# A hybrid decoder layer on one core: the sums of its twelve norms with ones as weights in four column groups, one filler and one split moved

## The chip, the core and the metric

The kernel runs on one core of one Trainium2 chip. Its time is the device time of one launch in microseconds (us), the median over runs. TensorE is called PE here, its weight loads PEld, VectorE DVE, ScalarE ACT, GpSimd POOL, and SyncE, which issues most of the transfers, SP.

## What is computed

One layer of a decoder for 1024 prompt tokens and 8 x 4 sample tokens, 1056 in all, with 1024 channels:

```python
def _rms(x, g):
    y = xf * lax.rsqrt(jnp.mean(xf * xf, axis=-1, keepdims=True) + EPS)
    return (y * g)

def _layer(x, p, ...):
    h = _rms(x, n_mix_pre)
    z = h @ w_in                       # q (8 heads x 64), k, v (2 x 64), u (4 x 128)
    a, k_state, v_state = attn_fn(q, k, v)         # 128 keys back, with sinks
    m, pool_state = _pool_mixer(u, pool_prev, pos0, w_pool, pool_scale)
    mix = jnp.concatenate([a, m], axis=-1) @ w_out
    x = x + _rms(mix, n_mix_post)
    f = _rms(x, n_ffn_pre)
    f = (jax.nn.silu(f @ w_gate) * (f @ w_up)) @ w_down
    x = x + _rms(f, n_ffn_post)
    x = x + jax.nn.sigmoid(x @ w_ple_gate) * (p @ w_ple)
    return x, k_state, v_state, pool_state
```

The eight results are the layer's output for prompt and sample, and the updated key, value and pooling buffers. All are float32.

## The kernel before, in words

Activations stand with channels on the 128 partitions and tokens along the free dimension. The 1056 tokens are cut into three groups (`g` = 0, 1, 2) of N = 352. A float32 product is made of three products in float32r: every operand is split into a high part (`hi`, a cast on ACT) and a rest (`lo`, a subtraction on DVE), by `split` (lines 172 to 174); `gemm` issues hi x hi, hi x lo and lo x hi for every 128 channels of the contraction. Nearly all matrix instructions come from one line, the helper `mm` (L128); `mt` (L122) turns a 128 x 128 block. Sums and scores are made in plain float32, which the trace shows as two records of PE for each instruction.

A norm needs, for each token, the sum of 1024 squares. DVE and ACT first add up eight channel blocks, so that `acc[g]`, 128 x 352, is left. `rstd_steps(acc)` (L355) then adds over the 128 partitions and spreads the result: PE sums (`b<-c,acc`), ACT takes the root (`sd`), DVE makes the reciprocal (L366), splits it into `hl` (L368, L369) and lays both parts into a tile `dg` (L375), and two products with a matrix of ones (`b<-dg,c`) bring 1/rms of all 352 tokens to all partitions. It runs twelve times: three norms at the start (`u_norm`), six in the channel sub-layer's input (`ffn_steps`, two for each group) and three in `x2_steps` near the end. The sums are three products, each with a 128-token piece of `acc` as weights and one column of ones as the moving side, the third piece overlapping the second. So token t stands on partition t mod 128 of column t // 128, and `diag`, three copies of the identity, puts it back in its place.

`yield a, b` in these steps hands over to the product stream: `turn` (L943) counts PE work, and a step goes on when the count has passed what it asked for (`a` divided by a share, plus `b`). At the start of the program the order on PE is fixed by hand (`pinned`), and the order on ACT and DVE in part (`fixed`); elsewhere the framework's scheduler orders each engine. [...]

The attention part mixes prompt and sample work (L890 to L922). `dscores` and `scores` make scores and their softmax (POOL multiplies by the reciprocal of the sum, L707), `dturned` turns the sample's weights in three banks, which ACT copies out (L818, L821), and `dvalues` multiplies them with the values. `filler(n)` takes n ready-made products of the output projection off a list, so that PE has work meanwhile; the first of them are `out_pool`, twelve matrix instructions and one ACT copy each (L844).

Late in the channel sub-layer `do_reload` (L1251) brings two tiles `fr` back from memory and splits them (`f_operand`), after waits of 50 and 70 in the count of `turn`.

Of the kernel before, what the change touches and what calls it, by code (L numbers as in the profile page):

```python
# [10 lines left out]
F32 = mybir.dt.float32  # L11
F32R = mybir.dt.float32r
AF = mybir.ActivationFunctionType
ALU = mybir.AluOpType
AX = mybir.AxisListType

P = 128
D = 1024
# [7 lines left out]
N = T // G  # L26
# [1 line left out]
OFF = tuple(N * g for g in range(G + 1))  # L28
NX = N

TB = 3
WIN = 128
NB = SEQ // WIN
PW = (2, 4, 8, 16)
# [28 lines left out]
def trunk_kernel(  # L63
# [33 lines left out]
    te, ve, se, ge = nc.tensor, nc.vector, nc.scalar, nc.gpsimd  # L97
# [4 lines left out]
    spool = ctx.enter_context(tc.tile_pool(name="spool", bufs=2))  # L102
# [5 lines left out]
    def nm(s):  # L108
        cnt[0] += 1
        return f"{s}{cnt[0]}"  # L110

    def act_tile(shape, dt=F32, s="a"):
        return apool.tile(shape, dt, tag="a", bufs=A_SLOTS, name=nm(s))

    def half(g, dt=F32, s="h"):
        return act_tile([P, 4, NS[g]], dt, s)
# [9 lines left out]
    def mm(*args, **kw):  # L126

        ins = te.matmul(*args, **kw)  # L128
        if pinned[0]:
            tc.keep_in_program_order(ins)  # L130

    def bank():
        return psum.tile([P, 512], F32, tag="b", name=nm("b"))
# [4 lines left out]
    def const(shape, src=None, s="c", dt=F32):  # L138
        t = cpool.tile(shape, dt, name=nm(s))
        if src is not None:  # L140
            nc.scalar.dma_start(t, src)
        return t
# [3 lines left out]
    ident = const([P, P])  # L146
    make_identity(nc, ident)

    diag = const([P, TB, P])
    lap = TB * P - N  # L150
    for i in range(TB - 1):
        ge.tensor_copy(diag[:, i, :], ident)
    ge.memset(diag[:, TB - 1, :], 0.0)
    ge.tensor_copy(diag[:, TB - 1, : P - lap], ident[:, lap:])
    ones = const([P, P])
    ge.memset(ones, 1.0)
    ones_r = const([P, P], dt=F32R)
# [1 line left out]
    epst = const([P, 1])  # L159
# [7 lines left out]
    def fix(ins):  # L167

        if fixed[0]:
            tc.keep_in_program_order(ins)  # L170
# [184 lines left out]
    def rstd_steps(acc):  # L355

        n = acc.shape[1]
        sm = bank()  # L360
        for i in range(TB):
            at = min(i * P, n - P)
            mm(sm[:, i : i + 1], acc[:, at : at + P], ones[:, 0:1], start=True, stop=True)
        sd = spool.tile([P, TB], F32, tag="sd", name=nm("sd"))
        fix(se.activation(sd, sm[:, :TB], AF.Sqrt, bias=epst, scale=1.0 / D))
        fix(ve.reciprocal(sd, sd))  # L366
        hl = spool.tile([P, 2, TB], F32R, tag="hl", name=nm("hl"))
        fix(ve.tensor_copy(hl[:, 0], sd))  # L368
        fix(ve.tensor_tensor(hl[:, 1], sd, hl[:, 0].bitcast(F32), op=ALU.subtract))  # L369
        dgs = []  # L370
        dg2 = act_tile([P, 2, TB, P], F32R, "dg")
        for h in range(2):
            dg = dg2[:, h]
            fix(
                ve.tensor_tensor(  # L375
                    dg, diag, hl[:, h].bitcast(F32).unsqueeze(2).to_broadcast([P, TB, P]), op=ALU.mult
                )
            )
            dgs.append(dg.rearrange("p i k -> p (i k)"))
        yield 6, 14  # L380
        ps = bank()
        for h in range(2):
            mm(ps[:, :n], ones_r, dgs[h][:, :n], start=h == 0, stop=h == 1)
        return ps[:, :n]

    def acc_rows():
        t = act_tile([P, 4, NX], s="acc")
        return [t[:, g, : NS[g]] for g in range(G)]
# [108 lines left out]
    n = 4 * NDEC * PST  # L497
# [51 lines left out]
    pinned[0] = True  # L549
    norms = [None] * G  # L550
    norms[0] = rstd_steps(acc1[0])
    for h in range(2):
        for c in range(4):
# [13 lines left out]
    for c in range(4):  # L567
        u_prod(c, 1, 1)
    norms[1] = rstd_steps(acc1[1])
    u_norm(norms[1], 1)  # L570
    for h in range(2):
# [4 lines left out]
    for c in range(4):  # L576
        u_evict(c, 1)
        se.copy(u_decode(c)[:, :, 0:PST], stt[:, c])
    split(wplh, wpll, wpl)
    norms[2] = rstd_steps(acc1[2])  # L580
    u_norm(norms[2], 2)
    for h in range(2):
# [42 lines left out]
    def project(i, j, g):  # L625
        ps = bank()
        gemm(ps[:, : NS[g]], ops8(weights(j), xs[g]))
        ve.tensor_tensor(qkv[i][:, OFF[g] : OFF[g + 1]], ps[:, : NS[g]], r1[g], op=ALU.mult)
# [17 lines left out]
    for c in range(4):  # L646
        n = NDEC * DSEQ
# [67 lines left out]
    def scores(b):  # L715


        t = act_tile([P, 8, WIN])
        nk = 2 * WIN if b else WIN
        lo = b * WIN + WIN - nk  # L720
        at = WIN * 4 // nk
        both = [[bank() for _ in range(4 // at)] for _ in range(2)]
        for c in range(4):
            for kv in range(2):
                rows = slice(64 * kv, 64 * kv + 64)
                i = c % at
                mm(
                    both[kv][c // at][:, i * nk : (i + 1) * nk],
                    qT[c][rows, b * WIN : (b + 1) * WIN],
                    kT[rows, lo : lo + nk],  # L730
                    start=True,
                    stop=True,
                )
        for kv in range(2):
            tk = t[:, 4 * kv : 4 * kv + 4, :]
            for i, ps in enumerate(both[kv]):
                tc_ = tk[:, i * at : (i + 1) * at, :]
                v = ps.rearrange("p (c k) -> p c k", k=nk)
                if b:
                    m = am[:, 0, :].unsqueeze(1).to_broadcast([P, at, WIN])  # L740
                    se.copy(tc_, v[:, :, :WIN])
                    ve.copy_predicated(tc_, m.bitcast(mybir.dt.int32), v[:, :, WIN:])
                else:
                    ve.tensor_tensor(tc_, v, m4(1), op=ALU.add)
            hs = slice(4 * kv, 4 * kv + 4)
            softmax(tk, 4, 0.125, skp[:, hs], nskp[:, hs])
        return t
# [62 lines left out]
    def dturned(t):  # L810
        pt = act_tile([P, NDEC + 1, P])
        for lo in (0, 4, 8):
            ps = bank()
            n = min(4, NDEC + 1 - lo)
            if lo < 8:
                for i in range(n):
                    mt(ps[:, i * P : (i + 1) * P], t[:, 0, (lo + i) * P : (lo + i + 1) * P])
                se.copy(pt[:, lo : lo + n, :], ps.rearrange("p (b c) -> p b c", c=P))  # L818
            else:
                mt(ps[: NDEC * DSEQ, :P], t[:, 0, 1024:])  # L820
                se.copy(pt[: NDEC * DSEQ, 8, :], ps[: NDEC * DSEQ, :P])  # L821
        return pt
# [23 lines left out]
    acc = acc_rows()  # L846
# [37 lines left out]
    def filler(n):  # L884
        for _ in range(n):
            if fill:
                f, *at = fill.pop(0)
                f(*at)
# [3 lines left out]
    td = dscores()  # L892
    t = scores(order[0])
    project(5, WQ[-1], 1)
    filler(1)
    od = bank()
    pts = [dturned(td[0])]
    filler(1)
    pts.append(dturned(td[1]))
    filler(1)  # L900
    ahead = scores(order[1])
    dvalues(pts, od)
    put(od, SEQ, NDEC * DSEQ)
# [52 lines left out]
    def chain(steps, wait=0, alone=False):  # L956

        chains.append([steps, now[0] + wait, alone])
# [46 lines left out]
    def f_operand(src, g):  # L1005
        hi, lo = half(g, F32R, "fh"), half(g, F32R, "fl")
        split(hi, lo, src)
        return hi, lo
# [242 lines left out]
    def do_reload():  # L1251
        def steps():
            ts = [half(2, s="fr") for h in range(2)]
            for h in range(2):
                nc.sync.dma_start(ts[h], fsd[h])
            yield 0, 50
            for h in range(2):
                fs[2][h] = f_operand(ts[h], 2)
                yield 10, 70

        chain(steps())

# [219 lines left out]
```

## Time and profile before

| what | before |
|---|---|
| median of 3 runs | 1089.85 us (1087.95 to 1090.51) |
| the profiled execution's own time | 1088.29 us |
| its span, first to last instruction | 1086.5 us |
| granted TensorE clock | 0.999 |
| PE busy | 1076.8 us (99%) |
| DVE, ACT, POOL busy | 873.2 (80%), 512.4 (47%), 283.2 us (26%) |

Busy times of PE are modelled from a pipeline: the records of two successive matrix instructions overlap, so the distance from start to start tells what one costs. In rows of the timeline the first number is the start in us, the second the time from the start of the first of the merged instructions to the end of the last; the shapes stand as rows*columns of the array in use, then partitions x elements of the moving side.

### The profile page before, as it was taken

The numbers are of one execution on the slowest core, as the hardware profiler recorded it, in microseconds if no ns is written. First come the engines' busy times: TensorE is split into PE (matmuls) and PEld (weight loads), VectorE is DVE, ScalarE is ACT, GpSimd is POOL, SyncE is SP. The second block draws the span as 40 slices with busy tenths as digits, with TensorE's granted clock in tenths as the row PEclk, the third lists the DMA queues.
The fourth block names the chain that finished last, engine by engine and source line by source line (L and its number), as shares of the span: only waits on it lengthen the run. The fifth ranks groups of instructions, "written<-read, shape, count | busy, mean of one in ns | idle before, by whom it ended". The sixth has DMA issues, their size and how long they took to land.

```text
span 1086.5 us, 17727 instructions
## 1 busy us (share of the span) xinstructions
PE 1076.8 (99%) x6867; PEld 1060.1 (98%) x6867; DVE 873.2 (80%) x1312; ACT 512.4 (47%) x877; POOL 283.2 (26%) x212
## 2 busy tenths in 40 slices
PE   9999999999999999999999999999999999999998
PEld 8999988899999999999999999999998999999998
DVE  6777478886878956796598898898899997969973
ACT  7423277774555533345543343443344365545531
POOL 0073032200000023436545445454442000022300
PEclk9999999999999999999999999999999999999999
DMA  8121311534553432322222222212234556553461
GB/s 296 59 72 39 120 50 40 188 143 141 190 184 130 136 117 78 131 78 78 78 79 78 83 74 85 91 59 97 79 112 161 170 179 224 182 210 125 135 203 60
DMA packets 43572, 131.27 MB, mean 121 GB/s; under 512 B 5060, under 2 KB 15588, under 8 KB 43488
## 3 DMA queue, kind: packets, MB, share of 16 engines
q1 hardware_dynamic: 42160, 128.38, 34.7%
q10 hardware_dynamic: 1328, 1.77, 0.5%
q8 instruction: 54, 0.88, 0.3%
q14 instruction: 30, 0.25, 0.1%
HBM read 114.25 MB, written 15.87 MB: 120 GB/s over the span
## 4 chain that ended last, share of the span: by engine, by line
PE 95%; DVE 3%; POOL 1%; ACT 1%; issue 1%; DMA 0%; SPq 0%; DVEq 0%; POOLq 0%; ACTq 0%
PE b L128 94%; PE b L122 1%; POOL wr L1058 1%; DVE sl L174 1%; DMA xr<-in_x_dram 0%; DVE hp L174 0%; DVE a L805 0%; DVE ap L1228 0%; ACT a L701 0%; DVE wl L174 0%; DVE hf L1133 0%; POOL a L707 0%; DVE w L174 0%; ACT sh L173 0%; DVE fl L174 0%
## 5 line engine op out<-in xcount | busy, mean ns | idle before, releaser
L1058 POOL TENSOR_TENSOR wr<-wr,wr 128x512 f32<-128x512 f32 x108 | 174.0, 1625 | 482.2 <-DMA wr<-in_w_gu_dram 242.3
L173 ACT CAST wh<-wr 128x1024 fp32r<-128x1024 f32 (+1 forms) x138 | 142.1, 1031 | 164.3 <-PE b L128 92.2
L174 DVE TENSOR_TENSOR wl<-wr,wh 128x1024 fp32r<-128x1024 f32 (+1 forms) x138 | 168.1, 1219 | 51.4 <-ACT wh L173 35.4
L128 PE MATMUL b<-fh,wh 128*128 128x352 f32 x624 | 201.5, 323 | 0.0
L128 PE MATMUL b<-fh,wl 128*128 128x352 f32 x624 | 200.0, 320 | 0.0
L128 PE MATMUL b<-fl,wh 128*128 128x352 f32 x624 | 199.9, 320 | 0.0
L173 ACT CAST sh<-wr 128x1024 fp32r<-128x1024 f32 x72 | 75.7, 1051 | 138.0 <-POOL wr L1058 131.9
L128 PE MATMUL b<-fh,sh 128*128 128x352 f32 x416 | 134.3, 323 | 0.0
L128 PE MATMUL b<-fl,sh 128*128 128x352 f32 x416 | 133.2, 320 | 0.0
L128 PE MATMUL b<-fh,sl 128*128 128x352 f32 x416 | 133.2, 320 | 0.0
L174 DVE TENSOR_TENSOR sl<-wr,sh 128x1024 fp32r<-128x1024 f32 x72 | 97.5, 1356 | 36.1 <-ACT sh L173 18.2
L128 PEld LDWEIGHTS b<-fl,wh 128*128 128x128 f32 x624 | 117.4, 188 | 0.0
L128 PEld LDWEIGHTS b<-fh,wh 128*128 128x128 f32 x624 | 117.0, 188 | 0.0
L128 PEld LDWEIGHTS b<-fh,wl 128*128 128x128 f32 x624 | 116.9, 187 | 0.0
L128 PE MATMUL b<-h,wh 128*128 128x352 f32 x480 | 105.6, 326 | 0.6 <-ACT h L426 0.6
L128 PE MATMUL b<-hid,wh 128*128 128x352 f32 x416 | 99.6, 322 | 0.0
L128 PEld LDWEIGHTS b<-h,wh 128*128 128x128 f32 x480 | 82.4, 190 | 1.6 <-ACT h L426 0.9
L1058 POOL TENSOR_TENSOR wr<-wr 128x512 f32<-128x512 f32 x36 | 51.0, 1416 | 105.9 <-DVE w L174 105.9
L128 PEld LDWEIGHTS b<-fl,sh 128*128 128x128 f32 x416 | 78.2, 188 | 0.0
L128 PEld LDWEIGHTS b<-fh,sh 128*128 128x128 f32 x416 | 78.0, 188 | 0.0
L128 PEld LDWEIGHTS b<-fh,sl 128*128 128x128 f32 x416 | 77.9, 187 | 0.0
L128 PE MATMUL b<-hp,sh 128*128 128x352 f32 x320 | 76.7, 322 | 0.8 <-DVE p L1085 0.6
(195 smaller groups left out, 2245.7 us busy)
## 6 DMA issues: line engine op xcount, KB each, us to landing
wr<-in_w_gu_dram SPq DMA_DIRECT2D x88, 512.0 KB, 3.3
wr<-in_w_dn_dram SPq DMA_DIRECT2D x40, 512.0 KB, 3.2
wr<-in_w_pg_dram SPq DMA_DIRECT2D x16, 512.0 KB, 3.5
x<-in_x_dram SPq DMA_DIRECT2D x6, 704.0 KB, 9.9
x1d<-x SPq DMA_DIRECT2D x6, 704.0 KB, 3.6
x<-x1d SPq DMA_DIRECT2D x6, 704.0 KB, 5.7
out_y_dram<-yo SPq DMA_DIRECT2D x24, 176.0 KB, 1.9
wr<-in_w_out_b_dram SPq DMA_DIRECT2D x8, 512.0 KB, 3.3
```

The costliest lines, as they stand in the source:

```text
L122: ins = te.transpose(out, src, ident)
L128: ins = te.matmul(*args, **kw)
L173: fix(se.copy(hi, src))
L174: fix(ve.tensor_tensor(lo, src, hi.bitcast(F32), op=ALU.subtract))
L1058: ge.tensor_tensor(out, a, b, op=op)
```

## The change

Three edits.

1. In `rstd_steps` the roles are swapped. The weights are now 32 columns of ones, and `acc` moves, in four pieces of w = 88 tokens; piece j goes to columns 32j to 32j+31 of the array, so its sums stand on partitions 32j to 32j+31 of PSUM, 88 of them in each row. Root, reciprocal and split work on 88 elements a partition, where there were 3. `dg` is the product of `lead` (one on partition 32j of column j, else zero), spread over 88 elements, with the 88 values, spread over four pieces: 352 elements where there were 384. POOL makes `lead` with four copies of one column, where it cleared and filled `diag`.
2. One `filler(1)` that stood behind the second `dturned` stands ahead of the first.
3. The waits in `do_reload` are 90 and 30, where they were 50 and 70.

```diff
-    diag = const([P, TB, P])
-    lap = TB * P - N
...
+    lead = const([P, 4])
+    for j in range(4):
+        ge.tensor_copy(lead[:, j : j + 1], ident[:, 32 * j : 32 * j + 1])
...
         n = acc.shape[1]
+        w = n // 4
         sm = bank()
-        for i in range(TB):
-            at = min(i * P, n - P)
-            mm(sm[:, i : i + 1], acc[:, at : at + P], ones[:, 0:1], start=True, stop=True)
-        sd = spool.tile([P, TB], F32, tag="sd", name=nm("sd"))
-        fix(se.activation(sd, sm[:, :TB], AF.Sqrt, bias=epst, scale=1.0 / D))
+        for j in range(4):
+            mm(sm[32 * j : 32 * j + 32, :w], ones[:, :32], acc[:, j * w : (j + 1) * w], start=True, stop=True)
+        sd = spool.tile([P, w], F32, tag="sd", name=nm("sd"))
+        fix(se.activation(sd, sm[:, :w], AF.Sqrt, bias=epst, scale=1.0 / D))
         fix(ve.reciprocal(sd, sd))
-        hl = spool.tile([P, 2, TB], F32R, tag="hl", name=nm("hl"))
+        hl = spool.tile([P, 2, w], F32R, tag="hl", name=nm("hl"))
...
-        dg2 = act_tile([P, 2, TB, P], F32R, "dg")
+        dg2 = act_tile([P, 2, 4, w], F32R, "dg")
+        at_row = lead.unsqueeze(2).to_broadcast([P, 4, w])
         for h in range(2):
             dg = dg2[:, h]
-            fix(
-                ve.tensor_tensor(
-                    dg, diag, hl[:, h].bitcast(F32).unsqueeze(2).to_broadcast([P, TB, P]), op=ALU.mult
-                )
-            )
+            part = hl[:, h].bitcast(F32).unsqueeze(1).to_broadcast([P, 4, w])
+            fix(ve.tensor_tensor(dg, at_row, part, op=ALU.mult))
...
     project(5, WQ[-1], 1)
-    filler(1)
+    filler(2)
     od = bank()
     pts = [dturned(td[0])]
     filler(1)
     pts.append(dturned(td[1]))
-    filler(1)
     ahead = scores(order[1])
     dvalues(pts, od)
...
-            yield 0, 50
+            yield 0, 90
             for h in range(2):
                 fs[2][h] = f_operand(ts[h], 2)
-                yield 10, 70
+                yield 10, 30
```

Lines stand one to seven places earlier in the changed kernel (L844 is L838 there, L818 is L812).

The first place is ACT in the attention part, from the copy of the first filler's result (`y`, from PSUM bank `b`) on; 32x128 and 128x512 are the copies of the turned blocks into `a`, and `wh` is the cast of the next weights. Before:

```order
L844 COPY y_1287<-b_1443 128x352
L698 ACTIVATE es_1406<-es_1406 128x4
L701 ACTIVATE a_1366,sm_1409<-a_1366,nmx_1404 128x128 x4
L818 COPY a_1458<-b_1459 128x512
L818 COPY a_1458<-b_1465 128x512
L821 COPY a_1458<-b_1471 32x128
L844 COPY y_1287<-b_1474 128x352
L818 COPY a_1488<-b_1489 128x512
L818 COPY a_1488<-b_1495 128x512
L821 COPY a_1488<-b_1501 32x128
L173 CAST wh_1918<-wr_1225 128x1024
L844 COPY y_1285<-b_1504 128x352
```

The same place on ACT in the changed kernel:

```order
L838 COPY y_1290<-b_1446 128x352
L692 ACTIVATE es_1409<-es_1409 128x4
L695 ACTIVATE a_1369,sm_1412<-a_1369,nmx_1407 128x128 x4
L838 COPY y_1290<-b_1460 128x352
L169 CAST wh_1921<-wr_1228 128x1024
L812 COPY a_1475<-b_1476 128x512
L812 COPY a_1475<-b_1482 128x512
L815 COPY a_1475<-b_1488 32x128
L838 COPY y_1288<-b_1491 128x352
L812 COPY a_1505<-b_1506 128x512
L812 COPY a_1505<-b_1512 128x512
L815 COPY a_1505<-b_1518 32x128
```

A second copy of a filler and the cast of the weights now stand ahead of all copies of the turned blocks; the last of these, the smaller of 32x128, moves from ahead of the cast to the end of the group. The same instructions are in both.

The second place is DVE at the fourth norm, the first of `ffn_steps`, from the reciprocal on (`y_1286` and `y_1289` are the sum of the two halves of the output projection, which waits for a product of PE). Before:

```order
L366 RECIPROCAL sd_2524<-sd_2524 128x3
L368 CAST hl_2527<-sd_2524 128x3
L863 TENSOR_TENSOR y_1286<-y_1286,b_2533 128x352
L369 TENSOR_TENSOR hl_2527<-sd_2524,hl_2527 128x3
L375 TENSOR_TENSOR dg_2530<-c_82,hl_2527 128x384 x2
```

And in the changed kernel:

```order
L362 RECIPROCAL sd_2528<-sd_2528 128x88
L857 TENSOR_TENSOR y_1289<-y_1289,b_2537 128x352
L364 CAST hl_2531<-sd_2528 128x88
L365 TENSOR_TENSOR hl_2531<-sd_2528,hl_2531 128x88
L372 TENSOR_TENSOR dg_2534<-c_82,hl_2531 128x352 x2
```

Here the sum `y` moved ahead of the cast, so that three steps of the norm stand behind it where two did.

For the third edit neither ACT nor DVE nor SP has an instruction in another place: the casts `fh<-fr` are the 595th and 602nd rows of ACT in both. Behind the last norm, some thirty instructions of DVE and a dozen of ACT swap places with their neighbours.

More of the change, by code (lines that the diff above doesn't have):

```diff
@@ L29 @@
 NX = N
-TB = 3
 WIN = 128
@@ L147, in trunk_kernel @@
     make_identity(nc, ident)
-    diag = const([P, TB, P])
-    lap = TB * P - N
[L151 to L154, printed above, removed]
+    lead = const([P, 4])
+    for j in range(4):
+        ge.tensor_copy(lead[:, j : j + 1], ident[:, 32 * j : 32 * j + 1])
     ones = const([P, P])
```

## The prediction

> **What bounds the kernel now.** I read the page first: busy time by engine (part 1) and the chain that ended last (part 4).
>
> ```profile
> PE 1076.8 (99%) x6867; PEld 1060.1 (98%) x6867; DVE 873.2 (80%) x1312; ACT 512.4 (47%) x877; POOL 283.2 (26%) x212
> PE 95%; DVE 3%; POOL 1%; ACT 1%; issue 1%; DMA 0%; SPq 0%; DVEq 0%; POOLq 0%; ACTq 0%
> ```
>
> PE is dense and makes up 95% of the chain. So what PE issues less, or waits less, comes off the time one for one; work of DVE, ACT or POOL counts only where PE waits for it. Next, the waits of PE, where two rows matter here:
>
> ```profile
> PE b L128 <- DVE ap L1228: 1.7, 2, 1.5
> PE b L122 <- POOL a L707: 1.1, 1, 1.1
> ```
>
> The second is the place that the moved filler touches. The first is the largest wait for DVE, late in the channel sub-layer; the order of no engine changes there.
>
> **The sums on PE, what goes.** The timeline of the first norm on PE, with its neighbours:
>
> ```profile
> 25.24 0.72 PE L128 MATMUL b<-c,acc 128*128 128x1 f32 x6
> 25.82 1.53 PE L128 MATMUL b<-h,wh 128*128 128x352 f32 x8
> 27.19 0.81 PE L128 MATMUL b<-h,wl 128*128 128x352 f32 x4
> 28.15 1.44 PE L128 MATMUL b<-h,wh 128*128 128x352 f32 x8
> ```
>
> The row at 28.15 gives the pace of a product undisturbed: eight records in 1.44 us, the last lasting 0.32, so (1.44 - 0.32) / 7 = 0.16 us. From 25.24 to 27.19 stand the six records of the sums and eight such products: 1.95 - 8 x 0.16 = **0.67 us** for one norm. One column streams in no time; it is the weights, 128 columns for each record, that cost. Two norms follow each other directly:
>
> ```profile
> 274.02 1.39 PE L128 MATMUL b<-c,acc 128*128 128x1 f32 x12
> 275.52 0.32 PE L128 MATMUL b<-fl,wh 128*128 128x352 f32 x1
> ```
>
> One product stands between these two rows, so the pair costs 1.50 - 0.16 = 1.34 us.
>
> **What comes.** No 32-column groups stand in the trace of before, but 64-column groups (128*64) and halves of the rows (64*128) do, in the attention part:
>
> ```profile
> 132.43 0.81 PE L128 MATMUL b<-a,a 64*128 64x256 f32 x6
> 132.87 0.38 PE L128 MATMUL b<-a,a 64*128 64x256 f32 x2
> 133.18 0.43 PE L128 MATMUL b<-h,wh 128*128 128x352 f32 x1
> 133.18 0.30 PEld L128 LDWEIGHTS b<-h,wh 128*128 128x128 f32 x2 [0.33 <-DVE a L805]
> 148.49 1.01 PEld L128 LDWEIGHTS b<-a,a 128*64 128x64 f32 x32 [0.17 <-issue]
> 181.53 0.74 PE L128 MATMUL b<-a,a 128*64 128x512 f32 x2
> ```
>
> - Stream: three pairs of 256 columns start in 0.81 - 0.38 = 0.43 us, 0.215 a pair, 0.84 ns a column. 88 columns take 0.074 us, two records 0.148.
> - Changing the cut of the array: the last pair of 256 starts at 132.87 and streams until 133.085, but the full product starts at 133.18, 0.09 us later. A norm now pays this twice, in and out. [...]
> - Weights after such a change are loaded in the open: the second load starts at 133.18 + 0.30 - 0.19 = 133.29, so 0.11 us for 128 columns. For 32 columns I take 0.03 by proportion.
> - Groups beside each other: 32 loads of 64 columns take 1.01 us, 0.03 each, where one of 64 would take 0.055 by the same proportion, so two groups load at once. And two records of 512 columns are over in 0.74, which one behind the other would need 2 x 512 x 0.84 ns = 0.86 for streaming alone. So groups overlap. How far apart they start has two bounds: nearly nothing (the paired loads), or a group's two loads, 0.054 for 32 columns, three times over: 0.16. I take 0.02, by the 32 loads, which are the longer series.
>
> One norm: 0.09 + 0.03 + 0.148 + 0.02 + 0.09 + 0.11 = **0.49 us**, so 0.18 saved (0.04 at the other bound). The pair shares its changes of cut: 0.49 + 0.148 = 0.64, so 0.70 saved.
>
> **What the longer chain does.** Behind the sums stand one step of ACT and three small ones of DVE, now with 88 elements. The price of size, from the groups of instructions:
>
> ```profile
> L1085 DVE TENSOR_TENSOR p<-p,b 128x352 f32<-128x352 f32 x78 | 40.1, 514 | 13.2 <-PE b L128 12.6
> L1178 ACT ACTIVATE sl<-b 128x352 f32<-128x352 f32 x22 | 10.1, 457 | 3.0 <-PE b L128 3.0
> L365 ACT ACTIVATE sd<-b,c 128x3 f32<-128x3 f32 x12 | 3.1, 262 | 3.6 <-PE b L128 3.3
> L697 DVE TENSOR_TENSOR es<-c,nmx 128x4 f32<-128x4 f32 (+1 forms) x18 | 2.6, 153 | 0.1
> ```
>
> DVE: (514 - 153) / 348 = 1.04 ns an element, so 85 more cost 0.09 us in each step, 0.27 in three; the two `dg` lose 32 elements each, 0.07. ACT: (457 - 262) / 349 = 0.56 ns, so 0.05. The bounds: nothing at all if small steps are all fixed cost, or this. I take this, since these are the same instructions in the two sizes. PE waits for the result only where it has no other work; before, that happened once by over 0.1 us, at the third norm (49.29 below). Three norms are close:
>
> ```profile
> 24.66 1.38 ACT L436 ACTIVATE xr<-xr 128x1408 f32<-128x1408 f32 x1 [1.97 <-DVE h L428]
> 26.00 0.26 ACT L365 ACTIVATE sd<-b,c 128x3 f32<-128x3 f32 x1
> 26.79 1.02 DVE L375 TENSOR_TENSOR dg<-c,hl 128x384 fp32r<-128x384 f32 x2
> 27.67 0.38 PEld L128 LDWEIGHTS b<-dg,c 128*128 128x128 f32 x2
> 47.73 0.16 DVE L366 RECIPROCAL sd<-sd 128x3 f32<-128x3 f32 x1
> 49.29 0.19 PEld L128 LDWEIGHTS b<-dg,c 128*128 128x128 f32 x1 [0.19 <-DVE dg L375]
> 227.06 0.52 DVE L863 TENSOR_TENSOR y<-y,b 128x352 f32<-128x352 f32 x1 [1.38 <-PE b L128]
> 227.57 1.02 DVE L375 TENSOR_TENSOR dg<-c,hl 128x384 fp32r<-128x384 f32 x2
> 228.63 0.35 PEld L128 LDWEIGHTS b<-dg,c 128*128 128x128 f32 x2
> ```
>
> First norm: `sd` cannot start earlier, since ACT is busy with the squares until 26.0. The second `dg` ended at 27.81 and its load started at 27.67 + 0.38 - 0.19 = 27.86; now it ends 0.05 + 0.27 - 0.07 = 0.25 later and the load is in the open. PE loses **0.21 us** here (0.25 + 0.11 of load, less the 0.14 that lay between load and product), whatever the sums save. Third norm: DVE is behind (the reciprocal starts at 47.73, PE already waits), so the 0.27 - 0.07 = **0.20** comes straight on top. Fourth norm: the cast now stands behind `y`, which PE releases 0.18 earlier; `dg` then ends at 227.57 + 1.02 - 0.18 + 0.20 (the cast's place) + 0.20 (size) - 0.07 = 228.74, the load stays at 228.63 + 0.35 - 0.19 = 228.79, and the 0.18 is lost: **0**. At the other seven single norms and the pair I count the whole saving: 7 x 0.18 + 0.70 = **1.96 us**. The cover there is the products up to `b<-dg,c`; where it is gone, a norm is worth about 0.
>
> **The filler.** The stretch in question, from several engines' timelines:
>
> ```profile
> 138.84 0.32 PE L128 MATMUL b<-mh,wl 128*128 128x352 f32 x1
> 140.25 0.33 PE L122 MATMUL b<-c,a 128*128 128x128 f32 x1 [1.08 <-POOL a L707]
> 144.69 1.05 ACT L818 COPY a<-b 128x512 f32<-128x512 f32 x2
> 145.63 0.25 ACT L821 COPY a<-b 32x128 f32<-32x128 f32 x1
> 145.79 0.44 ACT L844 COPY y<-b 128x352 f32<-128x352 f32 x1
> 148.54 1.15 ACT L741 COPY a<-b 128x256 f32<-128x256 f32 x4
> 148.12 0.19 PEld L128 LDWEIGHTS b<-a,a 32*64 32x64 f32 x4 [0.33 <-issue]
> 149.53 0.43 PE L128 MATMUL b<-mh,wh 128*128 128x352 f32 x1
> ```
>
> PE stood from 138.84 + 0.16 to 140.25, 1.25 us. The moved filler, 12 x 0.16 = 1.92 us, fills this. But ACT, not PE, is late next: from 144.69 to 148.54 it goes without a pause through the copies of both turned tiles, two fillers' copies and the cast of weights, and all it does before hangs on POOL and DVE, not on PE. In the new order the same work lies in the same 3.85 us, with the last small copy of the turned blocks at its end: it starts at 148.54 - 0.16 (the distance of the small copy at 145.63 to its successor) = 148.38 and ends at 148.63. `dvalues` needs it. Before, its first products started together at 148.12; now the second of them starts at about 148.69, and the part up to 149.53, 1.41 us, moves to end at 150.09: **0.56 us lost**. Nothing later gives it back, since PE has no other wait in that part. The bounds are that and a gain of 1.25.
>
> **The rest.** `lead` for `diag` spares POOL work in the first 3 us, before PE has data: 0. The waits in `do_reload`: the order stays, 0. DVE's swaps behind the last norm stand where PE never waits: 0, at the price of a rival below.
>
> Sum: -1.96 + 0.21 + 0.20 + 0 + 0.56 = **-0.99 us**. The profiled execution took 1088.29 (span 1086.5), so it would take 1087.3. The median of the runs shown is 1.56 above that execution; I set the change against the median: 1089.85 - 0.99, **1088.9 us**, with its own range 1087.8 to 1090.1 (the upper end with 0.14 less saved at each of the seven and the pair).
>
> **Rivals.**
> 1. *The column groups run one after another* (the slower side). Then eight records stream for 8 x 0.074 = 0.59: a norm costs 0.09 + 0.03 + 0.59 + 0.09 + 0.11 = 0.91, 0.24 more than before; the pair 1.50, 0.16 more. With 7 x 0.24 + 0.16 + 0.32 (first norm: its sums now end 0.1 later) + 0.35 + 0.24 + 0.56 = 3.3 the time is 1093.1. It decides as soon as less than a third of the streams overlap. Against it: the rows at 148.49 and 181.53. [...] The row at 148.49, two column groups at once, disagrees for 64 columns; no run here shows 32.
> 2. *The filler does fill the gap*, because ACT gets to the copies earlier than its old timeline says: then -1.25 in place of +0.56, 1087.0 to 1087.1. For it: ACT's start at 144.69 follows steps of DVE stretched while POOL works, which may fall otherwise. Against: none of their order changes.
> 3. *The small steps hardly grow*: no stall at the three norms, each saves 0.18 but the third, which stays: -1.96 - 0.36 + 0.56 = -1.76, 1088.1.
> 4. *An eviction comes late behind the last norm*, where DVE's order changed. The nearest price is the wait for `ap` above, 1.5 to 1.7: 1090.5.
>
> **How the numbers follow.** Forecast 0.48, rivals 0.12, 0.22, 0.08, 0.10. About 0.2%, 2.2 us, is what a measurement of this kernel can tell from no change: faster is under 1087.7, slower over 1092.0. Faster: most of rival 2 (0.20) and the low ends of forecast and rival 3 (0.08). Slower: rival 1 and a little of rival 4: 0.15. The rest, 0.57, is the same. The range reaches from 1086.7, below rival 2, to 1091.5, above rival 4, and leaves rival 1 out.
>
> **What would show it.** In the timeline, four groups of 32 whose eight records end within 0.25 us of the first, and 0.49 between the products around them; if 0.9, rival 1. Loads of `dg` waiting at the first and third norm by 0.2 and 0.4. At about 139 to 141 no wait for POOL, and at 145 to 149 waits of PE for ACT's copies, the next filler starting near 150.1 less what is saved ahead; if near 148.3, rival 2. A wait of PE behind 1000 would be rival 4. I would be wrong altogether if DVE's place in the stretch with `ap` shifted.

## The result, and the profile after

The changed kernel takes **1092.37 us** (median of 12 runs, 1090.77 to 1095.51) against 1088.86 us of before (12 runs beside them, one of which took 3789.48 us; a median does not feel it): ratio 1.0034, 95% interval 1.0026 to 1.0042. It is slower by 3.5 us. The forecast was 1.0 us faster, the range ended at 1091.5. The forecast of 1088.9 was set against the median of three runs, 1089.85; with twelve, before itself takes what was forecast for after.

The profiled execution of after took 1091.78, its span is 1090.0. First the busy times on its page:

```profile
PE 1079.7 (99%) x6891; PEld 1058.0 (97%) x6891; DVE 878.9 (81%) x1312; ACT 512.9 (47%) x877; POOL 281.8 (26%) x212
```

PE is idle for 1090.0 - 1079.7 = 10.3 us, before for 1086.5 - 1076.8 = 9.7. So of the 3.5 us only 0.6 are waits. The rest stands in PE's busy time, although the twelve sums became cheaper. The place shows in the busy times by stretch, here one stretch of 120 us in the channel sub-layer, first of before, then of after (columns: PE busy and its records, then PEld, DVE, ACT, POOL, the granted clock, the share of the transfers):

```profile
460.00:580.00 120.00, 120.00 (x757) 120.00 (x756) 95.07 (x120) 59.41 (x95) 56.67 (x35) 1.00 0.24 80
```

```profile
460.00:580.00 120.00, 120.00 (x752) 120.00 (x751) 94.35 (x119) 59.98 (x96) 54.05 (x35) 1.00 0.24 80
```

PE never pauses in either, the clock is full in both, all its work there is full products of 352 columns, and yet it gets through five fewer. A record lasts two starts, so about two more reach into the window: 120 / 755 = 0.1589 us a product before, 120 / 750 = 0.1600 after. The starts in the two traces show it sharper: six products (a period after which the distances repeat) take 953.3 ns in before and 960.0 in after, from 340 to 817 us, without a drift. That is 3.33 us in this stretch alone.

Before has a slower stretch of its own, behind the reloads, and its own trace tells:

```profile
842.00:876.00 34.00, 34.00 (x213) 34.00 (x212) 32.45 (x47) 15.35 (x26) 0.00 (x0) 1.00 0.49 166
342.00:376.00 34.00, 34.00 (x216) 34.00 (x215) 33.00 (x37) 18.66 (x22) 0.00 (x0) 1.00 0.42 140
```

34 / 211 = 0.1611 us a product against 34 / 214 = 0.1589. There are three steady **rhythms** of dense products: 953, 960 and 967 ns for six. In the traces of before and after PE changes from one to another only where the series of products is broken: by a wait, by the sums, or by a few products of the same size that read other tiles. So it goes in both at the products of the pooling mixer (`b<-mh,a`, nine at a time): 967 ns before the first nine (at 80.5 us in before), 960 behind them, 953 behind the second nine (at 93.4 us).

Now the places that the change touches. The sums, at the first norm and at the pair, from the timeline of PE in after:

```profile
25.02 0.36 PE L127 MATMUL b<-acc,c 128*32 128x88 f32 x8
25.31 1.55 PE L127 MATMUL b<-h,wh 128*128 128x352 f32 x8
...
274.76 0.32 PE L127 MATMUL b<-fh,wl 128*128 128x352 f32 x1
275.01 0.51 PE L127 MATMUL b<-acc,c 128*32 128x88 f32 x16
275.46 0.43 PE L127 MATMUL b<-fh,wh 128*128 128x352 f32 x1
275.72 0.32 PE L127 MATMUL b<-fl,wh 128*128 128x352 f32 x1
```

Eight records are over in 0.36 us: the four groups run beside each other. The pair costs 275.72 - 274.76 - 2 x 0.16 = 0.64 us.

The small steps behind them at the third norm, from the timelines of DVE and PE in after; then the groups of reciprocals (instructions, busy time, mean ns of one), of after and of before:

```profile
48.01 0.69 DVE L362 RECIPROCAL sd<-sd 128x88 f32<-128x88 f32 x1
48.73 0.20 DVE L364 CAST hl<-sd 128x88 fp32r<-128x88 f32 x1
48.97 0.25 DVE L365 TENSOR_TENSOR hl<-sd,hl 128x88 fp32r<-128x88 f32 x1
49.14 0.95 DVE L372 TENSOR_TENSOR dg<-c,hl 128x352 fp32r<-128x352 f32 x2
49.81 0.77 PE L127 MATMUL b<-dg,c 128*128 128x352 f32 x2 [0.48 <-ACT wh L169]
```

```profile
L362 DVE RECIPROCAL sd<-sd 128x88 f32<-128x88 f32 x12 | 8.2, 693 | 2.2 <-ACT sd L361 2.2
```

```profile
L366 DVE RECIPROCAL sd<-sd 128x3 f32<-128x3 f32 x12 | 1.9, 169 | 2.6 <-ACT sd L365 2.6
```

The reciprocal costs (693 - 169) / 85 = 6.2 ns an element, six times what I charged; the cast costs next to nothing more (medians 205 ns for 88 elements and 169 for 3). PE waits for `dg` at 49.81 (the row names ACT's cast, on which these products do not depend; the first of the two `dg` is done about half-way through the 0.95 us from 49.14).

What PE waits for in after, by line (us in total, times, the longest), and then the stretch of the moved filler on PE:

```profile
PE b L127 <- DVE ap L1221: 1.7, 2, 1.5
PE b L127 <- DVE dg L372: 0.9, 2, 0.5
PE b L127 <- ACT a L812: 0.7, 1, 0.7
PE b L127 <- ACT y L838: 0.3, 1, 0.3
```

```profile
146.10 0.70 PE L127 MATMUL b<-a,a 64*128 64x256 f32 x2 [0.29 <-ACT y L838]
147.52 3.55 PE L127 MATMUL b<-a,a 64*128 64x256 f32 x50 [0.73 <-ACT a L812]
151.00 0.43 PE L127 MATMUL b<-mh,wh 128*128 128x352 f32 x1
```

The wait for POOL's `a` is gone, and two waits for ACT's copies stand in its place.

Product by product, the starts in after against those in before give the account (us; a plus is lost):

| place | forecast | measured |
|---|---|---|
| up to the first norm (start of the program) | 0 | -0.30 (+0.37 in a second execution) |
| first norm | +0.21 | +0.76 (+0.38 in a second execution) |
| third norm | +0.20 | +0.59 |
| seven single norms, sums | -1.26 | -1.31 |
| pair | -0.70 | -0.69 |
| fourth norm | 0 | -0.13 |
| filler | +0.56 | +0.17 |
| tenth norm (first of `x2_steps`; the expectations below call it the seventh single norm), wait for dg | 0 | +0.92 |
| reloads and waits for `p` and `ap`, 817 to 840 us | 0 | -0.32 |
| rhythm, 340 to 817 us | not thought of | +3.33 |
| rhythm, 840 to 875, 910 to 995, behind the last norm | not thought of | -0.47, +0.55, +0.55 |
| sum (whole shift 3.5) | -0.99 | +3.65 |

Not in the table are a slower rhythm of after between 229 and 274 us, +0.24, and the products right behind several norms, -0.03 to -0.10 each; with these the account comes to the 3.5. Without the four rhythm terms, 3.96 us together, the change would be worth -0.3 to -0.5 us: no change. Of these terms only +3.33 and the +0.55 between 910 and 995 us came in a second execution of both kernels as well; the others differ between executions of one program (see the end).

### The profile page after: what moved, and what is told of

Its sections match the earlier page's. It is cut to its first block, busy times and chain, and to the rows that moved or that the text cites. A ratio compares the mean times of both kernels' runs of the same rounds, so it can differ in the third digit from the quotient of the medians.

```text
span 1090.0 us, 17775 instructions
## 1 busy us (share of the span) xinstructions
PE 1079.7 (99%) x6891; PEld 1058.0 (97%) x6891; DVE 878.9 (81%) x1312; ACT 512.9 (47%) x877; POOL 281.8 (26%) x212
## 4 chain that ended last, share of the span: by engine, by line
PE 87%; DVE 7%; DMA 2%; issue 2%; ACT 1%; POOL 0%; SPq 0%; DVEq 0%; ACTq 0%; POOLq 0%
PE b L127 86%; DVE wl L170 1%; DMA xr<-in_x_dram 1%; PE b L121 1%; DVE ap L1221 1%; DVE ap L1228 1%; DMA a<-in_p_dram 1%; DVE sl L170 1%; POOL wr L1051 0%; DVE acc L848 0%; DVE hp L170 0%; DMA c<-in_gains_dram 0%; ACT wh L169 0%; DVE fl L170 0%; ACT xr L430 0%
## 5 line engine op out<-in xcount | busy, mean ns | idle before, releaser
L170 DVE TENSOR_TENSOR wl<-wr,wh 128x1024 fp32r<-128x1024 f32 (+1 forms) x138 | 172.8, 1254 | 48.3 <-ACT wh L169 28.5
```

Of the source, the lines that this page charges most:

```text
L170: fix(ve.tensor_tensor(lo, src, hi.bitcast(F32), op=ALU.subtract))
```

## The experiments

**Which part, and is it chance?** Sums alone (filler and split set back), filler alone, and both kernels once more.

> Only the sums are changed; filler and split stand as before. In the trace of the changed kernel six successive full products take 960 ns through most of 335 to 824 us, in that of before 953 ns: 72 products in 11.52 against 11.44 us, 3.4 us over the stretch. Theory A (this rhythm of PE comes with the new sums, whatever else stands): 960 ns again in the long stretch and a time of 1092 us, 1.003 of before. Theory B (the rhythm is a chance of each execution, nothing to do with the sums): any of the two rhythms, and times that scatter over both, 1088.5 or 1092. Theory C (the moved filler shifts the program against something else and so sets the rhythm): 953 ns and 1088.5 us. In all cases the sums of a norm cost PE 0.49 us instead of 0.67, and dg is waited for at the first, third and seventh single norm, since the reciprocal of 88 elements takes 0.70 us and not 0.26.

> Only the filler is moved; sums as before. Theory A (the new sums bring the slower rhythm): 953 ns for six products from 335 to 818 us, and 1089.0 us, since the move of the filler alone is worth +0.2 us (1.25 us of gap filled, 1.6 us of new waits for ACT's copies, some of it given back by 156 us). Theory C (the filler sets the rhythm): 960 ns and 1092 us. Theory B (chance): either.

> The changed kernel once more, nothing edited. Theory A (the rhythm belongs to the program): 960 ns for six products in the long stretch again and 1091 to 1093 us. Theory B (chance of an execution): a trace with 953 or 967 ns there is as likely, and the times scatter between 1088 and 1096.

> The kernel before once more, nothing edited. Theory A: 953 ns in the long stretch again and 1088 to 1090 us, ratio 1.000. Theory B: 960 or 967 ns in some executions, with times up to 1096.

Measured: sums only 1091.68 us, ratio 1.0026 (1.0016 to 1.0035); filler only 1088.91, 1.0000 (0.9991 to 1.0009); after again 1091.85, 1.0030 (1.0019 to 1.0042); before again 1088.82, 0.9996 (0.9987 to 1.0005). The same stretch, sums only and then filler only:

```profile
460.00:580.00 120.00, 120.00 (x752) 120.00 (x751) 93.40 (x119) 59.88 (x96) 55.80 (x35) 1.00 0.24 80
```

```profile
460.00:580.00 120.00, 120.00 (x757) 120.00 (x757) 95.21 (x120) 59.68 (x96) 57.26 (x35) 1.00 0.24 80
```

After again has x752, before again x757. So in this stretch the rhythm belongs to the program (theory A against B), and it comes with the edit of `rstd_steps` (against C). The filler is worth nothing that can be measured. The third edit was not run alone, but sums only does without it, and the shift between 817 and 840 us is -0.30 us there, as against -0.32 in after.

**The sums or what stands behind them?** The rhythm turns slow at 334.4 to 334.6 us in all these traces with the new edit, and what stands there is the two products of `dg`; the sums of this norm stand 4.2 us earlier, at 330.19 in after, and between the two PE still has 953 ns. Two crosswise kernels, a kernel without reciprocals, and one with everything moved in memory:

```diff
# new_sums_old_dg: before, with
-        for i in range(TB): ... mm(sm[:, i : i + 1], acc[:, at : at + P], ones[:, 0:1], ...)
+        for j in range(4):
+            mm(sm[32 * j : 32 * j + 32, :w], ones[:, :32], acc[:, j * w : (j + 1) * w], ...)
# old_sums_new_dg: after, with the first of these loops, and
-        fix(se.activation(sd, sm[:, :w], AF.Sqrt, ...))
+        fix(se.activation(sd, sm[:, 0:1].to_broadcast([P, w]), AF.Sqrt, ...))
# no_recip: after, with
-        fix(ve.reciprocal(sd, sd))
+        fix(ve.tensor_copy(sd, sd))
# after_shift: after, with behind lead
+    room = cpool.tile([P, 132], F32, name="room")      # and a memset of its first column by POOL
```

> Before with one edit: the sums in four column groups; the root, the small steps and dg as before, on the first three columns of the sums alone, so that the norms are not the reference's. Theory S (the records of the sums, with their change of the array's cut, set the slower rhythm of the products behind them): 960 ns for six products from 335 to 820 us, so +3.9 us of rhythm against about -2.5 us at the sums (0.18 a norm, 0.65 the pair): 1090.2 us. Theory D (the new dg, two products out of a tile of pitch 352, or the room in memory that went with diag, sets it): 953 ns, and only the saving is left: 1086.4 us, ratio 0.998.

> After with one edit: the sums as before (three products with one column), their first column spread to 88 for the root, all behind it as in the changed kernel, so that the norms are not the reference's. Theory S: 953 ns in the long stretch; left are the waits for dg at the first, third and seventh single norm (0.97, 0.79 and 0.9 us) and no saving: 1091.3 us. Theory D: 960 ns there and 1095 us.

> After with the reciprocal of 88 elements replaced by a copy of 88, so that the norms multiply by the root. If the reciprocal (0.70 us against 0.17 for 3 elements) is what PE waits for at the first, third and seventh single norm, the waits shrink by 0.49 us each, 1.5 us together: 1090.5 us with the 960 ns unchanged. If the waits come from engines that are late anyway, they stay and the time is 1092.

> After with 528 unused bytes per partition taken behind lead, so that all tiles of weights and activations lie 528 bytes higher (diag's going moved them 1520 bytes down, which is 528 up in a raster of 2048). Theory of addresses: another rhythm in the long stretch, 953 or 967 ns, 1088.5 or 1095.5 us. Theories S and D of the stream: 960 ns and 1092 us.

Measured: new sums with old `dg` 1085.49 us, ratio 0.9974 (0.9964 to 0.9983); old sums with new `dg` 1094.95, 1.0059 (1.0043 to 1.0075); without reciprocals 1090.73, 1.0017 (1.0007 to 1.0027); moved by 528 bytes 1091.68, 1.0028 (1.0018 to 1.0038), with x752 in the stretch. The first two in the stretch:

```profile
460.00:580.00 120.00, 120.00 (x757) 120.00 (x757) 96.15 (x122) 59.34 (x95) 55.33 (x34) 1.00 0.24 80
```

```profile
460.00:580.00 120.00, 120.00 (x752) 120.00 (x752) 93.36 (x118) 60.17 (x96) 56.79 (x35) 1.00 0.23 75
```

The slow rhythm stays where everything is moved by 528 bytes (four times 128 and 16); the raster of 2048 bytes in that expectation was my assumption, and no run shows one. Theory S, mine until then, falls: the change of the array's cut does not slow the products behind it. The new sums alone are 0.26% faster than before, 2.8 us by the ratio; `dg` and the steps ahead of it bring the slow rhythm with either kind of sums. (The 1094.95 of the old sums met the expected 1095 in part by luck: the wait of 0.9 us expected at the tenth norm did not come.) The reciprocal's part is as expected: without it the third norm lies 0.10 us behind before and not 0.59, the first 0.11 ahead. The trace without reciprocals also tells writing from reading: DVE has written both halves of `dg` by 334.01 us, the twelve products up to the first of `dg` at 334.42 still take 954 ns for six, and those behind it 960.

**What about `dg`?** Its products read the same 352 columns. Only the place of the second half differs: 384 elements behind the first in before, 352 in after.

```diff
# dg_384: after, with
-        dg2 = act_tile([P, 2, 4, w], F32R, "dg")
+        dg2 = act_tile([P, 2, 384], F32R, "dg")      # dg = dg2[:, h, : 4 * w]
# before_dg_352: before, with
-        dg2 = act_tile([P, 2, TB, P], F32R, "dg")
+        dg2 = act_tile([P, 768], F32R, "dg")         # dg = dg2[:, h * n : h * n + TB * P]
```

> After with one edit: the two halves of dg lie 384 elements apart, as in before, instead of 352; the products read the same 352. No instruction moves. Theory P (where the second dg product reads sets the rhythm of all products behind it): 953 ns for six products from 335 to 822 us and behind 920, so about 3.9 us less than after: 1088.2 us, ratio 0.9995 of before. Theory Q (something else that came with the new small steps, the room in memory or the time at which dg arrives): 960 ns and 1092 us.

> Before with one edit: the second half of dg begins 352 elements behind the first instead of 384 (the first half's last 32, which nobody reads, are written over). Theory P: 960 ns in the long stretch and 1092 us or more, as slow as the changed kernel, with the old sums. Theory Q: 953 ns and 1089 us.

Measured: dg_384 1087.37 us, ratio 0.9987 (0.9978 to 0.9996); before_dg_352 1094.03, 1.0051 (1.0038 to 1.0063). The stretch, in this order:

```profile
460.00:580.00 120.00, 120.00 (x757) 120.00 (x756) 95.91 (x121) 59.43 (x95) 54.48 (x35) 1.00 0.25 80
```

```profile
460.00:580.00 120.00, 120.00 (x752) 120.00 (x751) 92.09 (x118) 60.28 (x96) 56.04 (x35) 1.00 0.23 75
```

Theory P holds both ways: 32 elements of distance between two halves of a tile, with no instruction of the changed kernel moved, turn 1.0034 into 0.9987. Nor do the instructions of PE, ACT, DVE or POOL change their order. (In before_dg_352 the overlap of the halves also lets other steps of DVE slip in between; a wait of 0.9 us for `dg` at the fourth norm is part of its 5 us.)

**Which property of the place?** Counted in pieces of 128 bytes from the tile's start, the halves lie at 0 and 12 in before, at 0 and 11 in after. Four kernels with others, and two with everything 128 bytes higher:

```diff
# dg_416, dg_448: dg2 = act_tile([P, 2, 416 or 448], ...)
# dg_both_32:     dg = dg2[:, 32 + 384 * h : 32 + 384 * h + 4 * w]
# dg_352_from_32: dg = dg2[:, 32 + 352 * h : 32 + 352 * h + 4 * w]
# after_shift_128, dg_384_shift_128: room = cpool.tile([P, 32], F32, name="room") behind lead
#                 (and a memset of its first column by POOL); dg's tile in the both_32 and from_32 kernels: [P, 832]
```

> After with the halves of dg 416 elements apart, 1664 bytes, 13 times 128 (352 is 11 times, 384 is 12 times 128 bytes, 3 times 512). Theory E (even multiples of 128 bytes give the quick rhythm, odd ones the slow): 960 ns for six products from 335 to 822 us and 1091.5 us. Theory F (the farther the better, at least 384): 953 ns and 1087.5. Theory G (multiples of 512 bytes alone are quick): 960 ns.

> After with the halves 448 elements apart, 1792 bytes, 14 times 128 and not a multiple of 512. Theory E: 953 ns and 1087.5 us. Theory F: 953 ns. Theory G: 960 ns and 1091.5 us.

> After with the halves 384 elements apart, but both 32 elements (128 bytes) farther into the tile. If the distance of the halves decides: 953 ns and 1087.5 us. If the place of the second half in its tile decides (now 13 times 128 bytes from its start): 960 ns and 1091.5 us.

> After with the halves 352 elements apart as there, but both 32 elements farther into the tile, so that the second begins at 384. If the distance decides: 960 ns and 1091.7 us. If the place of the second half decides: 953 ns and 1087.5 us.

> After with 128 unused bytes per partition taken behind lead, so that every tile of weights and activations, dg and the products' operands alike, lies 128 bytes higher. If it is the absolute place of dg's second half that decides (it comes from an odd to an even multiple of 128): 953 ns for six products from 335 to 822 us and about 1088 us. If it is its place against the operands of the products around it, which move along: 960 ns and 1091.7 us.

> The kernel with the halves of dg 384 elements apart, and every tile 128 bytes higher as well. Absolute place decides: 960 ns and 1091.5 us. Place against the other operands decides: 953 ns and 1087.5 us.

| kernel | sums | halves at | records, 460 to 580 us | us | ratio to before |
|---|---|---|---|---|---|
| dg_416 | new | 0, 13 | 752 | 1091.60 | 1.0030 (1.0016 to 1.0044) |
| dg_448 | new | 0, 14 | 757 | 1087.59 | 0.9995 (0.9984 to 1.0005) |
| dg_both_32 | new | 1, 13 | 752 | 1092.84 | 1.0046 (1.0030 to 1.0062) |
| dg_352_from_32 | new | 1, 12 | 757 | 1088.87 | 1.0005 (0.9995 to 1.0016) |
| after_shift_128 | new | 0, 11, all + 1 | 752 | 1091.93 | 1.0029 (1.0017 to 1.0042) |
| dg_384_shift_128 | new | 0, 12, all + 1 | 758 | 1087.18 | 0.9993 (0.9983 to 1.0004) |

The two that tell distance from place, dg_both_32 and dg_352_from_32; their tiles have one size, 832 elements, so that only the place of the second half differs:

```profile
460.00:580.00 120.00, 120.00 (x752) 120.00 (x751) 92.56 (x118) 60.52 (x96) 56.47 (x36) 1.00 0.23 77
```

```profile
460.00:580.00 120.00, 120.00 (x757) 120.00 (x757) 95.16 (x119) 60.69 (x96) 56.36 (x35) 1.00 0.24 80
```

Theory E holds, theories F and G fall: with the second half at an even piece of its tile the stretch is quick, at an odd one slow. For this stretch it is the place of the second half, not the distance, and not the absolute place, since one piece more ahead of all tiles changes nothing. Elsewhere the first half counts too: from about 917 to 998 us six products take 953 ns with an even and 960 with an odd second half, but 967 in both kernels whose first half lies at 1. The products around read tiles whose channel blocks lie 352 elements apart, so that their place is even and odd by turns, three products each; that would make a period of six. That is argued from the layout, not shown; and why two products set the rhythm of three thousand is not shown either.

**A better version.**

```diff
# hybrid: before, with rstd_steps(acc, wide); wide at nine norms: the new sums and steps,
# ident's columns 0, 32, 64, 96 for lead, sd in the second half of hl;
# at all twelve dg2 = act_tile([P, 2, 384]); else as before
-    norms[1] = rstd_steps(acc1[1])
+    norms[1] = rstd_steps(acc1[1], True)
...     # both of ffn_steps: True; x2_steps: g > 0
```

> A version meant to beat both, from before: the new sums with their 88-element steps at nine norms, where nobody waits for dg; the old ones at the first and third and at the seventh single norm, where the longer reciprocal was waited for in after; dg's halves 384 apart everywhere. Theory P: 953 ns nearly throughout; saved are 0.18 us at seven single norms and 0.65 at the pair, 1.9 us: 1086.9 us, ratio 0.998, and less if the 967 ns between sums and dg go too. Theory Q: 960 ns and 1090.5 us.

Measured: 1086.26 us, ratio 0.9976 (0.9966 to 0.9985): 2.6 us faster than before by the ratio, and 6 us under the changed kernel's 1092.37, which was measured in other rounds. Records in the stretch: 758. PE's waits name no `dg`, those of its weight loads 0.6 us in three.

## Why the prediction was wrong

- **PE issues less, so the time falls one for one: the step that failed.** I read the pace of a product, 0.16 us, from eight of them, and held it to be the same in both kernels. There are more than 6000. A pace 0.7% slower over 477 us costs 3.3 us, more than all terms of my sum. The sum had no term for it. The rows at 342 and 842 us of before show two paces at full clock and without pauses; I had not asked for them, and no rival of mine covered it. With the old pitch of `dg` alone (dg_384) the same change is 0.13% faster, 1.4 us by the ratio, near the -0.99; that is partly luck, since there too the small steps cost more and the filler less than forecast.
- **The sums**: right. 0.49 us a norm and 0.64 the pair were forecast, the seven single norms save 1.31 us in place of 1.26, the pair 0.69 in place of 0.70. The groups do run side by side. Rival 1 gives 1093.1, close to the result, but its mechanism is refuted: eight records in 0.36 us. The pair's sixteen records take 0.51 us.
- **The small steps**: mis-sized. I priced all three steps of DVE at 1.04 ns an element, by an addition of two sizes, and called them the same instructions. The reciprocal takes 6.2 ns, six times the price of an addition; why, no run here shows. Third norm +0.59 in place of +0.20; without the reciprocal +0.10. No row of before had a reciprocal of more than 4 elements, but with the shapes kept apart it had two sizes:

```profile
L705 DVE RECIPROCAL sm<-sm 128x4 f32<-128x4 f32 x16 | 2.8, 173 | 0.3
L705 DVE RECIPROCAL sm<-sm 128x1 f32<-128x1 f32 x2 | 0.3, 154 | 0.2 <-DVE sm L704 0.2
```

(173 - 154) / 3 = 6.3 ns an element, from few and short instructions, and yet the price that was measured. My price did not use it.

- **The cover at the tenth norm** held no longer in after: 0.92 us. In the eleven executions with these steps (all with the new sums and the new `dg`) the shift there lies between 0 and 1.3 us. In all nineteen traces the reciprocal, or the copy in its place, starts 14.5 us behind ACT's cast of `p`, which waits for the landing of `in_p_dram` (1.50 us in before, 2.54 in after). In the eleven PE waits 0 to 0.03 us where this cast starts at least 8.5 us ahead of the sums, 0.92 at 7.6 us (after) and 1.3 at 7.2: later by a microsecond, longer by a microsecond. With the old steps a cast 7.4 us ahead (hybrid) cost 0.17. So the longer chain used up the margin, and the transfer sets how much is missing; why it lands when it does is not shown.
- **The fourth norm**: -0.13 in place of 0: most of the 0.18 saved at the sums was kept.
- **The filler**: mechanism right, one step wrong. The gap of 1.25 us is filled, the waits for ACT's copies come, and the next filler starts 151.00 - 149.53 = 1.47 us later than before, having been 0.87 late ahead of it: 0.60 lost, forecast 0.56. "Nothing later gives it back" was wrong: until 159.46, before 158.42, 0.43 is made up, since two pairs of value products that ran one after the other in before start together. The steps of DVE that rival 2 called stretched are in both traces: the addition to `sm` on 128x1 (L704) takes 1.72 us at 138.49 in before, 1.71 of them while POOL works, and 0.15 at 137.55 without it; in after again 1.72, at 139.41. Alone, the move measured 1.0000.
- **The reloads, the late eviction**: no cost came from the reloads, as forecast, and the late eviction of rival 4 did not come.

## What to carry to other kernels

Where PE is dense, its pace between starts is a number to read by itself, stretch by stretch, in both kernels: here one nanosecond on a product was worth more than all that the edits saved. A tile that a product reads has a place as well as a size; when a layout changes, try the old pitch before judging the change. An instruction that grows in elements is priced by its own operation in two sizes, with the shapes kept apart, and if only one size stands in the trace, by a bound that can hurt.

## What the runs showed of the hardware

- Dense products of 352 columns have three steady paces at a granted clock of 1.00: 158.9, 160.0 and 161.1 ns a product. The place of one operand, even or odd in pieces of 128 bytes, chose between the first two: from 460 to 580 us the nineteen traces have 757 or 758 records with an even place and 752 with an odd one. Between before and after the difference lasts 477 us.
- In other stretches executions of one program differ. Before again has the quick rhythm between 842 and 876 us, where before has the slowest (x213 above):

```profile
842.00:876.00 34.00, 34.00 (x216) 34.00 (x215) 32.02 (x46) 14.77 (x25) 0.00 (x0) 1.00 0.53 180
```

After and after again differ from 229 to 254, from 889 to 911, and here behind the last norm, where before has x380:

```profile
1010.00:1070.00 60.00, 60.00 (x377) 60.00 (x376) 50.46 (x76) 25.32 (x37) 9.56 (x5) 1.00 0.48 153
```

```profile
1010.00:1070.00 60.00, 60.00 (x374) 60.00 (x373) 51.16 (x77) 26.07 (x38) 10.67 (x6) 1.00 0.49 155
```

60 / 375 = 0.1600 and 60 / 372 = 0.1613 us: the middle pace and the slowest for the same program. So something that differs between executions has a part there, and it stays open what.

- Four column groups of 32 with 88 moving columns each start within 0.02 us, and the whole, with both changes of the cut, costs 0.49 us where three products of one column cost 0.67. There the six records start 0.11 us apart, as do their weight loads of 128 columns.
